# The attention branch as seven quadrant products, and the pooling's moving sums by transfers

## The chip, the cores and the metric

One core of a Trainium2 chip runs the whole block. The metric is the device time of one execution in microseconds (us), the median over the runs shown. Five engines work beside each other, each through its own row of instructions: TensorE (PE, matmuls, with its weight loads as PEld), VectorE (DVE), ScalarE (ACT), GpSimd (POOL) and SyncE (SP), which here only issues transfers (DMAs). An instruction that waits holds up everything behind it in its engine's row.

## The reference

The block mixes a pooling part and an attention part through sigmoid gates, and an MLP follows. All sizes are 1024 (sequence and model), the branches are 512 wide.

```python
def _multiscale_pool(u, w_pool, pool_scale):          # windows w = 2, 4, 8, 16, a group of 128 channels each
    ...
        pooled.append((upper - lower) / count)        # mean over the last min(t + 1, w) rows
    diff = pooled - u
    mixed = jnp.einsum('bsgc,gcd->bsgd', diff, w_pool)
    return mixed.reshape(B, S, POOL_WIDTH) * pool_scale

h = _rmsnorm(x, g_mix_pre[l])
proj = h @ w_in[l] + b_in[l]
u_pool, q, k, v, gates = jnp.split(proj, IN_SPLITS, axis=-1)
y_pool = _multiscale_pool(u_pool, w_pool[l], pool_scale[l])
y_attn = _sliding_window_sink_attention(q, k, v, sinks)   # after a partial rotary embedding
g_pool, g_attn = split(sigmoid(gates))                    # 1024 columns each
merged = g_pool * (y_pool @ w_branch_pool[l]) + g_attn * (y_attn @ w_branch_attn[l])
x = x + _rmsnorm(merged @ w_out[l], g_mix_post[l])
x = x + _rmsnorm(square(relu(_rmsnorm(x, ...) @ w_up[l])) @ w_down[l], ...)
```

## The kernel before

Activations lie with channels on the 128 partitions and the sequence along the free dimension, in tiles of 128x512 or 128x1024. Every product is made in three passes (`PASSES`): each operand is split into a rounded high part and the rest, the high part by a cast on ScalarE (`split`, L101) and the low part by a subtraction on VectorE (L104), and high x high, high x low and low x high are added up in a bank of PSUM. Every matmul of the stages in question is 128x128 by 128x512.

The stages, by TensorE's time in the profile: norms and q, k, v up to 55 us; attention from 55 to 166, with the pooling's input u and the merged pooling weights computed in the gaps of attention; the gates from 166 to 319; the attention branch (L445, L447) to 362; the pooled branch to 406; the output projection to about 490; the MLP to the end.

**Attention.** `others()` is a generator of filler work. For each pooling group gi = 3, 2, 1, 0 it loads weights (`load_u`, `load_wb`, L572 and L582), makes u in two halves (`u_half`), stores u to DRAM (L611), and makes w_pool x w_branch_pool for that group (`wb_half`, stored at L627 to `wbp_dram`). SP also stores attention's output here (`y_dram`, L422), of which POOL adds a second part with an accumulating transfer (L424), and it loads the first gate weights (L475). POOL has small casts and differences of v besides (L103, L104, L330).

**Gates.** The class `Pairs` makes two column tiles of the gates at a time by seven Strassen products on quadrants. `gt.load` brings raw weights, `gt.operand(p, i)` makes the weight operand of product i (a sum or difference on VectorE, then a split). The first products are made from 166 to 210 us, and `rest(p, ...)` makes products 6, 7, 5, 4 and 3 of pair p, 60 matmuls, with an addition on VectorE behind each (L532, L539, L543, L546, L552), the scaling by the norm (L717, L713), the sigmoid on ScalarE (L709) and a store. Product 4 uses the bank of product 7 again, product 3 that of product 5. The operands of pair p are made in front of `rest(p)`.

**Branches.** `branch(w, rhs, base, m)` makes one column tile of 128 channels: a weight load and split, 24 matmuls into two banks (4 x 128 rows, 3 passes, 2 halves of the sequence), and two multiplications by the gates (L932). It runs eight times for attention and eight times for pooling. Attention's moving operand is loaded and split in `load_attn` during the last gate pair. Between the attention branch's tiles, `pool_part(gi)` loads u, adds the bias (L688), makes the moving sums by doubling, one addition of 128x1024 for w = 2 and four for w = 16 (L692, ten in all), subtracts u (L696, L698) and splits the result into `yphi` and `yplo`, the pooled branch's moving operand.

**Order.** Except inside blocks of `tc.manual_schedule`, which keep the order in which the code is written for the engines they name, a scheduler with a cost model orders the rows of PE, DVE and ACT. In attention and the first gates a hand-written interleaving (`fill`, `first`, `second`) decides. Tiles come from pools with a fixed number of buffers (`y`, `x`, `ga`, `bc` and others), so a tile waits until its buffer's last reader is done.

## Time and profile before

| | |
|---|---|
| median of 3 runs | 1109.25 us (1107.92 to 1109.52) |
| profiled execution, own time | 1109.43 us |
| its span | 1107.6 us |
| granted TensorE clock, mean | 0.998 |
| attention with its filler work | 55 to 166.3 us |
| gates: first products, then eight pairs | 166.3 to 209.8, 209.8 to 318.9 us |
| attention branch, pooled branch | 318.9 to 362.4, to 406 us |

The span is the profiled stretch of one execution; the execution's own time is some 2 us longer. Busy time is what an engine spent in instructions, without waits. In a list of groups a row gives line, engine, operation, tiles and count, then busy time and the mean of one in ns, then the idle time ahead of them and what ended it. In a timeline a row gives start and length, and a bracket, where there is one, the idle time before it and its releaser. "PEq", "SPq" and the like are an engine's issuing side.

### The profile page before, as it was taken

What the parts mean: (1) busy time and instruction counts of PE and PEld (TensorE: products, weight loads), DVE (VectorE), ACT (ScalarE), POOL (GpSimd) and SP (SyncE); (2) the same over time, 40 slices, a digit from 0 to 9 for tenths busy, and PEclk for the clock granted to TensorE, in tenths of its full rate; (3) what the DMA queues carried; (4) which work ended last, traced back from release to release, by engine and by line L of the source; (5) the groups of instructions that cost most, each with busy time, mean ns of one, the idle gap of its engine ahead of it and who ended that gap; (6) DMA issues with size and microseconds to landing.
All of it is one profiled execution on the core that took longest, in us unless ns stands there. A gap on an engine that the chain in (4) does not pass through costs nothing.

```text
span 1107.6 us, 13855 instructions
## 1 busy us (share of the span) xinstructions
PE 1097.7 (99%) x5108; PEld 907.5 (82%) x5108; DVE 807.1 (73%) x1175; ACT 547.6 (49%) x916; POOL 62.7 (6%) x107
## 2 busy tenths in 40 slices
PE   9999999999999999999999999999999999999997
PEld 7888788888888888878888888888888888888886
DVE  5578867899768796899878867666548944456596
ACT  7466656444432337587555654444434434344342
POOL 0344220000001120000000000000000000000000
PEclk9999999999999999999999999999999999999999
DMA  9406578355677581570457645445597535534673
GB/s 349 161 11 137 149 169 278 132 191 209 224 256 246 152 186 58 192 271 32 162 197 264 242 169 199 146 151 199 178 371 232 189 98 174 177 102 152 204 229 119
DMA packets 89747, 203.71 MB, mean 184 GB/s; under 512 B 8400, under 2 KB 21072, under 8 KB 89680
## 3 DMA queue, kind: packets, MB, share of 16 engines
q1 hardware_dynamic: 77536, 176.88, 48.0%
q10 hardware_dynamic: 5616, 19.66, 4.6%
q0 software_dynamic: 6528, 6.29, 4.0%
q8 instruction: 40, 0.66, 0.3%
q14 instruction: 27, 0.22, 0.1%
HBM read 147.23 MB, written 55.58 MB: 183 GB/s over the span
## 4 chain that ended last, share of the span: by engine, by line
PE 88%; DVE 5%; DMA 3%; ACT 2%; issue 2%; DVEq 0%; SPq 0%; ACTq 0%
PE mm L511 24%; PE at L511 16%; PE at L1406 16%; PE mm L1406 12%; PE mm L601 4%; PE mm L187 3%; PE mm L445 2%; PE at L196 1%; PE at L419 1%; PE mm L447 1%; PE sc L355 1%; PE sc L187 1%; DMA d<-spill_dram 1%; PE at L1048 1%; PE mm L1048 1%
## 5 line engine op out<-in xcount | busy, mean ns | idle before, releaser
L1406 PE MATMUL at<-ar,wh 128*128 128x512 f32 x744 | 169.6, 389 | 0.0
L1406 PEld LDWEIGHTS at<-ar,wh 128*128 128x128 f32 x744 | 139.6, 188 | 29.3 <-DVE ar L104 0.4
L104 DVE TENSOR_TENSOR wh<-raw,wh 128x1024 fp32r<-128x1024 f32 x53 | 64.8, 1223 | 99.4 <-ACT wh L101 99.4
L1406 PE MATMUL mm<-ar,wh 128*128 128x512 f32 x576 | 131.0, 389 | 0.0
L101 ACT CAST wh<-raw 128x1024 fp32r<-128x1024 f32 x53 | 55.8, 1053 | 146.7 <-PE at L1406 71.6
L1406 PEld LDWEIGHTS mm<-ar,wh 128*128 128x128 f32 x576 | 108.1, 188 | 22.4
L101 ACT CAST wh<-st 128x512 fp32r<-128x512 f32 (+1 forms) x97 | 61.6, 646 | 74.4 <-PE at L511 19.9
L104 DVE TENSOR_TENSOR wh<-st,wh 128x512 fp32r<-128x512 f32 (+1 forms) x97 | 68.8, 719 | 27.8 <-ACT wh L101 25.3
L511 PE MATMUL mm<-gr,wh 128*128 128x512 f32 x333 | 80.4, 391 | 0.0
L511 PEld LDWEIGHTS mm<-gr,wh 128*128 128x128 f32 x333 | 62.1, 188 | 13.1 <-DVE gr L1087 0.4
L511 PE MATMUL mm<-T,wx 128*128 128x512 f32 x288 | 67.6, 389 | 0.0
L511 PEld LDWEIGHTS mm<-T,wx 128*128 128x128 f32 x288 | 54.1, 188 | 11.2
L511 PE MATMUL at<-T,wx 128*128 128x512 f32 x252 | 59.1, 389 | 0.0
L511 PEld LDWEIGHTS at<-T,wx 128*128 128x128 f32 x252 | 47.3, 188 | 9.8
L511 PE MATMUL mm<-x,wh 128*128 128x512 f32 x240 | 55.2, 389 | 0.0
L511 PEld LDWEIGHTS mm<-x,wh 128*128 128x128 f32 x240 | 45.0, 188 | 9.4
L104 DVE TENSOR_TENSOR ar<-B,ar 128x1024 fp32r<-128x1024 f32 x37 | 45.1, 1219 | 4.0 <-ACT ar L101 3.9
L601 PE MATMUL mm<-x,wh 128*128 128x512 f32 x192 | 47.5, 395 | 0.0
L101 ACT CAST ar<-B 128x1024 fp32r<-128x1024 f32 x37 | 38.9, 1051 | 5.9 <-DMA B<-in_w_dn_dram 3.0
L601 PEld LDWEIGHTS mm<-x,wh 128*128 128x128 f32 x192 | 35.3, 188 | 7.7
L511 PE MATMUL at<-gr,wh 128*128 128x512 f32 x150 | 36.7, 390 | 0.0
L101 ACT CAST wx<-ws 128x512 fp32r<-128x512 f32 x30 | 18.6, 620 | 32.7 <-DVE ws L487 17.9
(384 smaller groups left out, 2162.4 us busy)
## 6 DMA issues: line engine op xcount, KB each, us to landing
raw<-f_dram SPq DMA_DIRECT2D x53, 512.0 KB, 3.7
f_dram<-g SPq DMA_DIRECT2D x30, 512.0 KB, 3.3
B<-in_w_dn_dram SPq DMA_DIRECT2D x24, 512.0 KB, 6.3
st<-in_w_up_dram SPq DMA_DIRECT2D x20, 512.0 KB, 4.1
st<-in_w_g_dram SPq DMA_DIRECT2D x18, 512.0 KB, 4.6
f_dram<-g ACTq DMA_DIRECT2D x17, 512.0 KB, 2.6
g<-spill_dram SPq DMA_DIRECT2D x16, 512.0 KB, 5.4
raw<-in_w_dn_dram SPq DMA_DIRECT2D x16, 512.0 KB, 4.7
```

The costliest lines, as they stand in the source:

```text
L101: act.copy(hi, src)
L104: eng.tensor_tensor(lo, src, f32(hi), ALU.subtract)
L187: pe.matmul(bq, xs_[k][n // 4][:, xh, n % 4 * P:(n % 4 + 1) * P], wq[k][:, h, :], start=k == 0 and j == 0, stop=k == NK - 1 and j == 2)
L196: pe.matmul(bkv_of(n), xs_[k][n // 4][:, xh, n % 4 * P:(n % 4 + 1) * P], wkv[k // 2][:, h, k % 2, :], start=k == 0 and j == 0 and not (joi ...
L355: pe.matmul(sb[:, kv, i, :nk], qt[r, qx, m * P:(m + 1) * P], kx[r, k0:k0 + nk], start=j == 0, stop=j == 2)
L419: pe.matmul(flat(yb), v[:, kv, :], flat(p[:, 4 * kv:4 * kv + 4]), start=j == 0, stop=j == len(mms) - 1)
L445: pe.matmul(bs[th], whi[:, k, :], rhs(k, hl, th), start=k == 0 and hl == 0, stop=False)
L447: pe.matmul(bs[th], wlo[:, k, :], rhs(k, 0, th), start=False, stop=k == nk - 1)
L511: pe.matmul(b, w[:, wh, kt, :], xo[kt][:, xh, :], start=not after and kt == 0 and j == 0, stop=kt == 3 and j == 2, skip_group_check=after)
L601: pe.matmul(b, (whi, wlo)[h][:, k, :], xr(k, xh, th), start=j == 0, stop=j == len(mms) - 1)
L1048: pe.matmul(bs[t], gop[i][kt // 2][gh][:, kt % 2, t * P:(t + 1) * P], wop[i][kt // 2][wh][:, kt % 2], start=not after and kt == 0 and j == ...
L1406: pe.matmul(bs[t], fo[fh][:, k2, t * P:(t + 1) * P], wo_[wh][:, k2, :], start=not after and s2 == 0 and k2 == 0 and j == 0, stop=s2 == NS ...
```

## The change

The attention branch is made by a class `Halves` as four weight pairs p of two column tiles, each by seven Strassen products on quadrants (two 128-row tiles of depth, 512 of the sequence). `first(p)` makes products 1 and 2, `rest(p)` makes 5, 6, 3, 7, 4. A product is 2 x 3 = 6 matmuls. The order in time is first(0), first(1), rest(0) with first(2) before its last product, rest(1) with first(3), rest(2), rest(3). In place of two multiplications for a column tile there are seven copies, additions and multiplications on ScalarE and VectorE for a weight pair (L978, L988, L991 copies on ScalarE; L981 to L1003 on VectorE). The moving operand's quadrants are combined on VectorE once (`combine`, L929, T1 to T4, 128x1024 each), and four sums of quadrant weights are made for each weight pair (`weights`, L947 to L950, 128x256 each).

The gates' operands are now made one pair ahead: `rest` calls `side()` after each addition, and a side step makes one operand of pair p + 1; in pairs 4 to 7 the side steps also load, combine and split the branch's operands (table `extra`). SP and POOL keep the written order there.

The pooling's moving sums are made by transfers between DRAM tiles while attention runs: u is stored twice (L619, L620), POOL adds a shifted copy by an accumulating transfer (`shifted`, L597), and for each further doubling SP copies the sum to a new tile first (L677). Eight of the ten additions are done in this way. `pool_load(gi)` then loads u and the sum, two tiles for a group, and `pool_split(gi)` does the remaining doubling, if any, the scaling by 1/w on ScalarE (L709), the subtraction and the split. The pooled branch (`pooled`) takes the first three groups for its first four column tiles before it needs the fourth group.

```diff
+    sum_dram = [[spill[i] for i in rows] for rows in ((20,), (21,), (22, 28), (23, 29, 30, 31))]
...
+    def shifted(gi, i):
+        src = sum_dram[gi][i - 1] if i else u_dram[gi]
+        pool.dma_start(sum_dram[gi][i][:, 1 << i:], src[:, :S - (1 << i)], accum_op=ALU.add)
...
             nc.sync.dma_start(u_dram[gi], u)
+            nc.sync.dma_start(sum_dram[gi][0], u)
...
             yield from u_half(gi, 0)
+            for g, i in {2: ((3, 0),), 1: ((3, 1), (2, 0)), 0: ((3, 2), (2, 1), (1, 0))}.get(gi, ()):
+                shifted(g, i)
...
             yield from u_half(gi, 1)
+            for g, i in {2: ((3, 1),), 1: ((3, 2), (2, 1)), 0: ((3, 3),)}.get(gi, ()):
+                nc.sync.dma_start(sum_dram[g][i], sum_dram[g][i - 1], max_dma_last_dim=4096)
...
-        while step < w:
-            t = place()
-            dve.tensor_tensor(t[:, step:], src[:, step:], src[:, :S - step], ALU.add)
...
+        act.activation(t, t, AF.Identity, bias=bias, scale=1.0 / w)
+        dve.tensor_tensor(u, t, u, ALU.subtract)
...
+    shifted(3, 3)
+    shifted(0, 0)
...
+        PRODUCT = {1: ("A11", "B11"), 2: ("A12", "B21"), 3: ("S4", "B22"), 4: ("A22", "T4"),
+                   5: ("S1", "T1"), 6: ("S2", "T2"), 7: ("S3", "T3")}
...
+        def rest(self, p, sides, between):
+            z, x, t, t2 = zg[self.base, p], self.x.pop(p), self.tmp.pop(p), g32([2, 512])
+            y = self.bank(p)
+            self.mm(y, p, 5)
+            act.copy(t2[:, 0], y)
+            sides[0]()
+            self.mm(x, p, 6, True)
+            act.copy(t[:, 0], x)
+            sides[1]()
+            self.mm(y, p, 3, True)
+            dve.tensor_tensor(t[:, 0], t[:, 0], y, ALU.add)
+            dve.tensor_tensor(z[1][:, 0], z[1][:, 0], t[:, 0], ALU.mult)
+            sides[2]()
+            self.mm(x, p, 7, True)
+            dve.tensor_tensor(t2[:, 0], t2[:, 0], x, ALU.add)
+            dve.tensor_tensor(z[1][:, 1], z[1][:, 1], t2[:, 0], ALU.mult)
+            sides[3]()
+            between()
+            self.mm(x, p, 4, True)
+            dve.tensor_tensor(z[0][:, 1], z[0][:, 1], x, ALU.mult)
...
+        extra = {(4, 2): lambda: w_todo.append(ba.weights(0)),
...
+                 (6, 0): lambda: ba.combine("T1", "B12", "B11", ALU.subtract, "B11"),
...
+        for p in range(4):
...
+            pool_load(p)
...
+            ba.rest(p, (nothing if p < 0 else lambda: w_next(p), nothing, lambda: w_split(p),
+                        lambda: pool_split(p) if p < 3 else None),
+                    (lambda: ba.first(p + 2)) if p < 2 else nothing)
...
+    for m in range(4):
+        pooled(m, range(3))
+    pool_split(3)
```

Lines move by up to some hundred in the changed kernel; a tile's number is its own in each program. SP's row in the second half of attention, before, from the store of the second pooling group to the first load of gate weights (`st<-in_w_g_dram`):

```order
L611 DMA spill_dram<-u_1106 128x1024
L422 DMA y_dram<-yt_1421 256x1x128 x2
L572 DMA st_1579<-in_w_u_dram 128x1024
L627 DMA wbp_dram<-wt_1338 128x8x128
L582 DMA st_1785<-in_w_bp_dram 128x1024
L611 DMA spill_dram<-u_1347 128x1024
L422 DMA y_dram<-yt_1589 256x1x128 x2
L475 DMA st_1875<-in_w_g_dram 128x1024
```

The same stretch of SP's row after; each L677 copies a sum and waits for POOL's accumulation into it:

```order
L620 DMA spill_dram<-u_1106 128x1024
L423 DMA y_dram<-yt_1422 256x1x128 x2
L576 DMA st_1583<-in_w_u_dram 128x1024
L677 DMA spill_dram<-spill_dram 128x1024
L636 DMA wbp_dram<-wt_1339 128x8x128
L677 DMA spill_dram<-spill_dram 128x1024
L586 DMA st_1794<-in_w_bp_dram 128x1024
L619 DMA spill_dram<-u_1348 128x1024
L620 DMA spill_dram<-u_1348 128x1024
L423 DMA y_dram<-yt_1593 256x1x128 x2
L677 DMA spill_dram<-spill_dram 128x1024
L476 DMA st_1887<-in_w_g_dram 128x1024
```

Three copies stand ahead of the first gate weights now, one behind the other.

VectorE's row in gate pair 6, before, from the addition behind product 6 (L532) to the last scaling (L713):

```order
L532 TENSOR_TENSOR z_2800<-z_2800,at_2928 128x512
L104 TENSOR_TENSOR ar_3016<-ws_3006,ar_3016 128x512
L539 TENSOR_TENSOR z_2927<-z_2800,at_2929 128x512
L543 TENSOR_TENSOR z_2927<-z_2927,at_2930 128x512
L546 TENSOR_TENSOR z_2927<-z_2800,at_2929 128x512
L717 TENSOR_TENSOR z_2927<-z_2927,rb_all 128x1024
L552 TENSOR_TENSOR z_2800<-z_2800,at_2930 128x512
L104 TENSOR_TENSOR wh_3166<-st_3163,wh_3165 128x512
L713 TENSOR_TENSOR z_2800<-z_2800,rb_all 128x512
```

The same pair after, to the addition behind product 4 (L548) and the quadrant sum behind it; L533, L541 and L544 are the additions behind products 6, 7 and 5, L929 the branch's quadrant sums, L105 low parts of splits, L492 a weight difference of the next pair:

```order
L533 TENSOR_TENSOR z_2857<-z_2857,at_2975 128x512
L105 TENSOR_TENSOR ar_3032<-ws_2991,ar_3032 128x512
L929 TENSOR_TENSOR q_2939<-q_2939,q_2903 128x1024
L541 TENSOR_TENSOR z_2974<-z_2857,at_2976 128x512
L492 TENSOR_TENSOR st_2859<-st_2859,ws_2991 128x512
L105 TENSOR_TENSOR wo_3081<-q_2964,wo_3080 128x1024
L544 TENSOR_TENSOR z_2974<-z_2974,at_2977 128x512
L105 TENSOR_TENSOR wh_3073<-st_2859,wh_3073 128x512
L105 TENSOR_TENSOR wh_2815<-st_2751,wh_2814 128x1024
L105 TENSOR_TENSOR ar_2817<-ws_2809,ar_2816 128x768
L548 TENSOR_TENSOR z_2974<-z_2857,at_2976 128x512
L929 TENSOR_TENSOR q_2964<-q_2964,q_2939 128x1024
```

Between the additions there now stand up to three operations of the branch's and the next pair's operands; four more rows of the pair follow (two scalings, L728 and L724, the addition L555, and a weight sum L947 of 128x256).

ScalarE's row in the branch, before, with pool_part's bias additions (L688) and the casts of splits (L101):

```order
L101 CAST yphi_3247<-d_3235 128x1024
L688 ACTIVATE d_3285<-d_3285,vec 128x1024
L101 CAST wh_3304<-st_3302 128x512
L688 ACTIVATE d_3378<-d_3378,vec 128x1024
L101 CAST yphi_3294<-d_3285 128x1024
L101 CAST wh_3346<-st_3344 128x512
```

And after, around weight pair 1's products 5 and 6, whose banks L988 and L991 copy out:

```order
L102 CAST wh_3345<-st_3235 128x1024
L701 ACTIVATE d_3241<-d_3241,vec 128x1024
L988 COPY g_3331<-mm_3332 128x512
L709 ACTIVATE d_3242<-d_3242,vec 128x1024
L991 COPY g_3214<-mm_3213 128x512
L102 CAST yphi_3290<-d_3241 128x1024
L701 ACTIVATE d_3327<-d_3327,vec 128x1024
L978 COPY g_3388<-mm_3387 128x512
```

The copies out of banks now stand between the pooling's activations (L701 adds the bias to u, L709 scales the sum).

More of the change, by code (lines that the diff above doesn't have):

```diff
@@ L523, in m2, with rest @@
             self.close_first(self.f0[p][:, :512], b)
-        def rest(self, p, f1, b6, b7, b5, done=(), then=None, b4=None):
+        def rest(self, p, f1, b6, b7, b5, done=(), side=lambda: None, b4=None):
             f0 = self.f0.pop(p)
@@ L532, in rest @@
             dve.tensor_tensor(u2, u2, b6, ALU.add)
+            side()
             if p in self.b1:
@@ L983, in merge, with split_pairs @@
+    gop, wop = {}, {}
+    def split_pairs(srcs, place, behind=None):
+        ops = [(place([2, 512]), place([2, 512])) for _ in srcs]
+        for hi, _ in ops if behind else ():
+            pool.tensor_copy(hi[:, 0, :1], behind[:, 0, :1])
+        for (hi, lo), t in zip(ops, srcs):
+            split(hi, lo, t)
+        return ops
     def merge(j):
@@ L988, in merged, with pooled @@
         return [zg[8, 2 * kh + j][th] for j in range(2)]
-    def x_place(shape):
-        return xp.tile([P] + shape, F32R, tag="x", name=nm("wo"))
+    def pooled(m, ks):
+        if m not in pw:
+            ws = stage([4, P])
+            nc.sync.dma_start(ws, wbp_dram[m])
+            t = wslot([2, 4, P])
+            split(t[:, 0], t[:, 1], ws)
+            tag = "mm" if m in (0, 1, 4, 5) else "at"
+            pw[m] = t, [bank(tag) for _ in range(2)]
+        t, bs = pw[m]
+        for k in ks:
+            for hw, hx in PASSES:
+                for th in range(2):
+                    pe.matmul(bs[th], t[:, hw, k, :], ysp[k][hx][:, th * 512:(th + 1) * 512],
+                              start=k == 0 and hw + hx == 0, stop=k == 3 and hw == 1, skip_group_check=True)
+    pw = {}
+    for m in range(4):
+        pooled(m, range(3))
+    pool_split(3)
+    gate_pair(0, 0)
+    gate_pair(0, 1)
     b11, b12 = merged(0, 1), merged(0, 0)
     for m in range(8):
-        branch(wbp_dram[m], lambda k, hl, th: ysp[k][hl][:, th * 512:(th + 1) * 512], 0, m)
+        if m == 4:
+            gate_pair(0, 2)
+        elif m == 6:
+            gate_pair(0, 3)
+        pooled(m, range(3, 4) if m < 4 else range(4))
+        z = zg[0, m // 2]
+        for th in range(2):
+            dve.tensor_tensor(z[th][:, m % 2], z[th][:, m % 2], pw[m][1][th], ALU.mult)
         if m == 4:
```

208 lines of the change are left out of this document (149 added, 59 removed).

## Prediction

> **What bounds the kernel now.** I read the busy shares first, then TensorE's waits, then the chain of waits, then the busy time stage by stage. The page's head:
>
> ```profile
> span 1107.6 us, 13855 instructions
> PE 1097.7 (99%) x5108; PEld 907.5 (82%) x5108; DVE 807.1 (73%) x1175; ACT 547.6 (49%) x916; POOL 62.7 (6%) x107
> ```
>
> TensorE (PE) is busy for 99% of the span. All its waits together, from the view of waits (total, times, longest), are under 4 us:
>
> ```profile
> PE mm L205 <- DVE zeros L183: 1.5, 1, 1.5
> PE sc L355 <- DVE s L364: 0.8, 2, 0.5
> ...
> PE mm L445 <- ACT wh L101: 0.2, 1, 0.2
> ```
>
> In the chain of waits (start, length) the gate stage is one gapless run of matmuls:
>
> ```profile
> 278.26 13.60 PE mm L511 x60
> 291.86 13.60 PE at L511 x60
> ```
>
> So 60 matmuls of 128x512 take 13.60 us, 0.2267 us each. Removing a matmul here saves that much, as long as the work beside it keeps up. How close that work comes is read by stage (length, then busy time of PE, PEld, DVE, ACT and POOL with counts, clock, DMA share, GB/s):
>
> ```profile
> core 0: us, PE busy (x) PEld busy (x) DVE busy (x) ACT busy (x) POOL busy (x), PEclk, DMA share, GB/s
> 55.00:166.30 111.30, 110.38 (x664) 90.51 (x663) 84.87 (x132) 68.06 (x214) 35.84 (x68) 1.00 0.51 116
> 224.00:308.00 84.00, 84.00 (x372) 69.57 (x371) 72.89 (x108) 38.02 (x51) 0.00 (x0) 1.00 0.65 219
> 306.00:361.50 55.50, 55.50 (x246) 45.96 (x245) 41.81 (x67) 16.11 (x18) 4.16 (x4) 1.00 0.77 247
> ```
>
> The rows are attention, six gate pairs, and the attention branch with the last gate pair. In the gate pairs VectorE is already busy for 87%, in the branch for 75%. The granted clock is 1.00 throughout and the change leaves TensorE as dense, so I leave it there.
>
> **Term 1, the matmuls: -5.44 us.** The attention branch in the groups of the window 318 to 363 us:
>
> ```profile
> L445 PE MATMUL mm<-yahi,wh 128*128 128x512 f32 x64 | 24.9, 389 | 0.0
> L445 PE MATMUL mm<-yalo,wh 128*128 128x512 f32 x64 | 24.9, 389 | 0.0
> L447 PE MATMUL mm<-yahi,wh 128*128 128x512 f32 x64 | 19.7, 389 | 0.0
> ```
>
> That is 192 matmuls. Seven products of six matmuls for each of four weight pairs are 168: 24 x 0.2267 = 5.44 us. The pooled branch keeps 192 (its order alone changes), so this is the only gain on TensorE.
>
> **Term 2, VectorE in the gate pairs: 0.** Durations by shape (busy, mean ns), then four consecutive starts in time:
>
> ```profile
> L104 DVE TENSOR_TENSOR wh<-st,wh 128x512 fp32r<-128x512 f32 x41 | 27.6, 685 | 7.9 <-ACT wh L101 7.7
> L692 DVE TENSOR_TENSOR t<-d 128x1023 f32<-128x1023 f32 x4 | 4.9, 1222 | 3.4 <-ACT d L688 3.4
> L932 DVE TENSOR_TENSOR g<-g,mm 128x512 f32<-128x512 f32 x30 | 19.2, 680 | 3.5 <-PE mm L447 3.5
> ...
> 292.74 1.22 DVE L717 TENSOR_TENSOR z<-z,rb_all 128x1024 f32<-128x1024 f32 x1
> 293.88 0.68 DVE L552 TENSOR_TENSOR g<-g,mm 128x512 f32<-128x512 f32 x1
> 294.47 0.68 DVE L104 TENSOR_TENSOR wh<-st,wh 128x512 fp32r<-128x512 f32 x1
> 295.08 0.68 DVE L713 TENSOR_TENSOR g<-g,rb_all 128x512 f32<-128x512 f32 x1
> ```
>
> Back to back a 1024-wide operation costs 1.14 us and a 512-wide one 0.60; on that line 768 comes to 0.87 and 256 to 0.33 (interpolated). The change puts four quadrant sums (L929), the splits of the branch's operands and of the first weight sums into pairs 4 to 7. The order's piece for pair 6 goes from eight 512s and one 1024, 8 x 0.60 + 1.14 = 5.9 us, to nine 512s, five 1024s, one 768 and one 256: 5.4 + 5.7 + 0.9 + 0.3 = 12.3 us of the pair's 13.60. Counted in the same way the pairs 3 to 7 need 11.4 to 12.9 us. This holds as an average; inside a pair, product 4 reuses the bank that the addition behind product 7 (L541) reads, and product 3 the bank of L544, with one product (12 matmuls, 2.72 us) between. Before, VectorE waited for TensorE at both:
>
> ```profile
> 300.05 0.69 DVE L543 TENSOR_TENSOR z<-z,at 128x512 f32<-128x512 f32 x1 [1.18 <-PE at L511]
> 302.77 0.69 DVE L546 TENSOR_TENSOR z<-z,at 128x512 f32<-128x512 f32 x1 [2.03 <-PE at L511]
> ```
>
> Walking the new order with these durations leaves at least 1.0 us before TensorE waits, least in pair 7. I take 0; bounds 0 and 3 us. The side steps are also what makes the operands one pair early, so none is late at a pair's start.
>
> **Term 3, waits inside the shorter branch: +1.2 us.** The branch now takes 168 x 0.2267 = 38.1 us. VectorE's list for it is 28 merges (28 x 0.60 = 16.8, priced by the L932 row's shape), weight sums and splits about 10, T4's split 1.1, and three pooling groups at two to three 1024s, about 7: 35 us, and it starts some 4 us behind the gates' end by the same walk. It has no slack to speak of, but it can run over: the pooled branch begins with 72 matmuls (16.3 us) that need no merge. The removed moving sums (eight of ten at 1.14, 9.1 us) and the four final combinations are what paid for the room.
>
> What bites is ScalarE, which now copies banks out between TensorE's products and has the pooling's activations queued in the same row. Its prices:
>
> ```profile
> L518 ACT COPY g<-mm 128x512 f32<-128x512 f32 x4 | 2.3, 587 | 3.2 <-PE mm L511 3.2
> L688 ACT ACTIVATE d<-d,vec 128x1024 f32<-128x1024 f32 x4 | 4.6, 1152 | 13.8 <-DMA d<-spill_dram 13.8
> L101 ACT CAST yphi<-d 128x1024 fp32r<-128x1024 f32 x4 | 4.2, 1046 | 8.3 <-DVE d L698 8.3
> ```
>
> For weight pair 1 the row is activation, copy (L988), activation, copy (L991): 1.15 + 0.59 + 1.15 + 0.59 = 3.48 us, while TensorE has two products of six between (2.72): it waits 0.76 us. In pair 2 a cast (1.05) takes an activation's place; part of it is done before, about 0.4 us stays (estimate by the walk). Together 1.2. Bounds: 0, if the activations run ahead, and 4 us, if a pooling load is also late (below).
>
> **Term 4, transfers in attention: 0.** Eight accumulating transfers by POOL (L597), four copies by SP (L677) and four more stores (L620) of 512 KB. What the trace has near (count, KB, us from issue to landing; the first from the branches, the others from the window 85 to 170 us), and the places in time:
>
> ```profile
> s<-in_w_o_dram POOLq DMA_DIRECT2D x8, 512.0 KB, 7.3
> y_dram<-yt POOLq DMA_DIRECT2D x14, 128.0 KB, 5.3
> spill_dram<-u SPq DMA_DIRECT2D x4, 512.0 KB, 3.9
> st<-in_w_g_dram SPq DMA_DIRECT2D x4, 512.0 KB, 4.9
> ...
> 118.89 0.46 POOL L330 TENSOR_TENSOR df<-vf,vf 128x128 f32<-128x128 f32 x1
> 140.19 0.33 SPq L475 DMA_DIRECT2D st<-in_w_g_dram  x1
> 158.67 1.18 ACT L101 CAST wh<-st 128x512 fp32r<-128x512 f32 x2
> 165.00 1.14 ACT L101 CAST wh<-st 128x512 fp32r<-128x512 f32 x2
> 166.13 4.24 PE L511 MATMUL mm<-x,wh 128*128 128x512 f32 x18
> ```
>
> The first accumulation stands behind L330 on POOL, so at 119.4. The first gate weights' load on SP, at 140.19 before, now stands behind the third copy, which needs the third accumulation of the widest group: accumulate, copy, accumulate, copy, accumulate. With A for an accumulation and C for a copy it issues at 119.4 + 3A + 2C. No row shows DRAM to DRAM; A lies between 5.3 and 10 (the 512 KB row with a third on top for the busier queues), C between 3.9 and 8.8 (a store and a load in series). I take A = 7.3, the only accumulation of this size, and C = 4.5, between store and load: 150.3, landing at 155.5, before ScalarE's cast at 158.67. The second load waits for one more accumulation: 157.6, landing at 162.8, before its cast at 165.00. Both hidden, 10 us later than now.
>
> The Trainium skill ("DMA: Bandwidth & Descriptors", section "Anatomy of one DMA — SWDGE (gpsimd) path") gives 2.0 us plus bytes over 436 GB/s for such a transfer, an estimate of 3.2 us for 512 KB. The trace differs, at 7.3; by the page's figure the chain would end some 12 us sooner, and the sum would be the same.
>
> **Term 5, the first gates: +0.3 us.** From 166 to 186 us the loads are what is late, and the transfers are dense:
>
> ```profile
> 178.00:182.00 4.00, 4.00 (x19) 3.30 (x18) 1.59 (x3) 2.61 (x4) 0.00 (x0) 1.00 1.05 406
> 179.39 0.62 ACT L101 CAST wh<-st 128x512 fp32r<-128x512 f32 x1 [3.59 <-DMA st<-in_w_g_dram]
> 183.26 0.62 ACT L101 CAST wh<-st 128x512 fp32r<-128x512 f32 x1 [1.18 <-DMA st<-in_w_g_dram]
> ```
>
> The last extra store and the last accumulations fall here: 0.5 MB is 1.3 us at 406 GB/s for each. The weights cast at 179.39 are used about 182.6, so some 2 us hide. Bounds 0 and 2; I take 0.3, near the lower end.
>
> **Sum.** -5.44 + 0 + 1.2 + 0 + 0.3 = -3.9 us. The profiled run took 1109.43 us (1.8 beside its span), 0.2 above the median of 1109.25, so against the runs: 1109.25 - 3.9 = 1105.3; with the walk's rounding I say 1105.2. I count less than 0.2% (2.2 us) as no change: 1107.0 to 1111.5.
>
> **Rivals.**
> *All hidden.* The copies' rows on ScalarE slide ahead, and the whole 5.44 shows: 1103.8. For it: ScalarE's 16.11 of 55.50 us in the branch. Against: the stack of 3.48 us.
> *The branch eats it.* A pooling load lands late, and the activation that waits for it stands in ScalarE's row ahead of copies that TensorE waits for. The chain of waits of before has one:
>
> ```profile
> 327.24 7.44 DMA d<-spill_dram
> ```
>
> I plan some 4 us; 3.4 us more, once, gives -0.5, 1108.7. For it: the pooling now loads eight tiles there and not four. Against: 2 MB more and 5.4 us less raise the 247 GB/s of the row above to about 315, under the 406 that a row of term 5 shows.
> *VectorE bounds the gate pairs.* If its operations take their full 0.68 and not 0.60, a pair of 12.9 us needs 14.6; three such pairs lose about 1 us each at L541 and L544: 1108.2. For it: the 12.3 of 13.60 us above. Against: 293.88 to 295.08, the starts 0.60 apart.
> *Slower: SP's queue holds the gate weights.* The second load's weights are wanted 12 matmuls after the gates' start, at 168.85; less a cast and a subtraction of 0.62 + 0.68 it must land by 167.5, 5.2 us after its issue. With 119.4 + 4A + 2C, all in series, that needs A under 8.5; from there each us of A costs 4, and the gain of 3.9 is gone at A = 9.4. At A = 11: 4 x 2.5 = 10 us late, 1115.2. For it: the POOL row of 128 KB already takes 5.3 us, and these accumulations read and write DRAM at a shifted, odd address. Against: the second load's extra accumulation overlaps the one ahead of it, which moves the point to A near 10.
> The Trainium skill ("SBUF — State Buffer", section "Who interferes with whom") speaks on this rival's side: transfers issued by GpSimd can starve while VectorE runs its doubled modes. No run here shows it. The trace leaves it open: in attention VectorE is busy for 84.87 of 111.30 us, and its 1024-wide operation costs 1.1 ns an element, no less than the 512-wide one, so no faster mode is seen there.
>
> **Numbers.** Forecast 0.52 (its own range 1104.3 to 1107.0), all hidden 0.13, branch eats it 0.12, VectorE bounds 0.08, SP's queue 0.15. Faster 0.65, same 0.20, slower 0.15. The range runs from 1103.0 (all hidden, less half of the 1.6 us by which the three runs differ) to 1111.0, which leaves out the last rival and little else.
>
> **What would show it.** After: 168 matmuls in the branch, gate pairs of 13.60 us in the chain, TensorE's new waits on ScalarE's copies (L988, L991) near 1 us in total, the gate weights' cast at about 158.7 and gates at 166. Wrong if TensorE waits at the first gates on weights, if L541 or L544 appear among its releasers, or if accumulations take over 8.5 us.

## The result, and the profile after

The changed kernel is slower: 1118.3 us (1115.82 to 1120.95, four runs) against 1109.38 (four runs), a ratio of 1.0082, 95% interval 1.0054 to 1.0111. I had forecast 1105.2, in a range that ended at 1111.0. The profiled execution is the lowest of the four, 1115.82 us with a span of 1114.0 against 1107.6, so 6.4 us of the 9 can be read from its trace.

TensorE's waits, which were under 4 us together before, have a new row after, by far the largest (the page's head, then that row of the view of waits):

```profile
span 1114.0 us, 13850 instructions
PE mm L512 <- ACT wh L102: 6.2, 2, 3.6
```

The chain of waits of after shows the place, at the gates' start, and behind it a dense stage as before:

```profile
159.84 14.68 DMA st<-in_w_g_dram
...
180.52 10.82 DMA st<-in_w_g_dram
...
235.31 13.60 PE mm L512 x60
```

The full gate pairs begin at 235.31 us instead of 223.86: 11.45 us lost in all. Of it 0.9 is there when the gates start (167.04 against 166.13), and nearly all of that since the first 10 us of the span, long before any changed instruction. From the gates' start to the first full pair it was 57.73 us before and is 68.27 now. TensorE's rows of after there, and the granted clock in the stretches behind its two waits (last columns: clock, DMA share, GB/s):

```profile
167.04 5.60 PE L512 MATMUL mm<-x,wh 128*128 128x512 f32 x24
175.27 13.20 PE L512 MATMUL mm<-x,wh 128*128 128x512 f32 x48 [2.62 <-ACT wh L102]
192.03 13.14 PE L512 MATMUL mm<-x,wh 128*128 128x512 f32 x49 [3.57 <-ACT wh L102]
...
175.27:178.00 2.73, 2.73 (x7) 2.11 (x8) 2.41 (x4) 1.99 (x3) 0.00 (x0) 0.50 1.06 255
192.03:200.00 7.97, 7.97 (x28) 6.12 (x29) 5.60 (x9) 3.74 (x7) 0.00 (x0) 0.80 1.05 344
```

The two waits are 6.19 us. The 48 matmuls behind the first took 13.20 us instead of 48 x 0.2267 = 10.88, the first 49 behind the second 13.14 instead of 11.11: another 4.35 us. Together that is 10.54 us, all of 68.27 - 57.73: the waits and the slower matmuls behind them are the whole loss. The granted clock, 0.50 over 2.73 us behind the first wait and 0.80 over 7.97 us behind the second, makes 0.50 x 2.73 + 0.20 x 7.97 = 3.0 us of the 4.35. The other 1.4 us are not the clock: in the run of plain shifted copies below it stayed at 1.00, and the 120 matmuls behind the wait there took 28.02 us instead of 27.20 (row in the last section). What makes these gaps was not looked into.

The branch itself does what the forecast said, in the windows of after for the gate pairs, the branch and the pooled branch:

```profile
235.31:330.50 95.19, 95.19 (x421) 78.82 (x421) 88.19 (x129) 43.86 (x56) 0.00 (x0) 1.00 0.61 218
330.50:368.60 38.10, 38.10 (x169) 30.97 (x168) 35.34 (x56) 24.00 (x32) 2.43 (x2) 1.00 0.74 244
```

TensorE is busy for all of 38.10 us, beside 35.34 us of VectorE. From the full pairs to the first MLP products in the chain of waits it was 492.81 - 223.86 = 268.95 us before and is 499.21 - 235.31 = 263.90: 5.05 us gained.

Why the weights came late, in SP's row of after (start, length of the issue), in ScalarE's casts that waited, and, last, in SP's row of before:

```profile
150.20 0.55 SPq L476 DMA_DIRECT2D st<-in_w_g_dram  x1
155.75 0.83 SPq L476 DMA_DIRECT2D st<-in_w_g_dram  x1
159.84 0.58 SPq L476 DMA_DIRECT2D st<-in_w_g_dram  x1
164.89 5.60 SPq L476 DMA_DIRECT2D st<-in_w_g_dram  x1
172.52 6.04 SPq L619 DMA_DIRECT2D spill_dram<-u  x1
...
165.91 1.14 ACT L102 CAST wh<-st 128x512 fp32r<-128x512 f32 x2
174.60 1.14 ACT L102 CAST wh<-st 128x512 fp32r<-128x512 f32 x2 [6.57 <-DMA st<-in_w_g_dram]
191.36 0.62 ACT L102 CAST wh<-st 128x512 fp32r<-128x512 f32 x1 [7.98 <-DMA st<-in_w_g_dram]
...
170.71 0.95 SPq L475 DMA_DIRECT2D st<-in_w_g_dram  x1
```

The two loads I had walked went out at 150.20 and 155.75 and were in time. The third goes out at 159.84, about when it did before, and takes 14.7 us to land, where the load took 4.9 before. Issuing itself takes 5.60 us at 164.89 and 6.04 at 172.52, so SP's queue is backed up. The fifth load, on which the second wait hangs, is late mainly because it went out late: at 180.52, where it went out at 170.71 before. SP spent most of the time between on the two long issues. Its landing took 10.8 us against 8.7.

The two queues' share of the 16 transfer engines from 110 to 200 us, before and then after (q1 is SP's, q0 POOL's; packets, MB, share):

```profile
q1 hardware_dynamic: 10199, 15.48, 54.5%
q0 software_dynamic: 3260, 1.57, 16.6%
...
q1 hardware_dynamic: 10924, 18.14, 58.8%
q0 software_dynamic: 4416, 5.76, 40.5%
```

POOL's queue grows by 24 points of 90 us, 21.5 us for the eight accumulations, about 2.7 us each of all 16 engines. With SP's it is 99% of the stretch, where it was 71%.

### The profile page after: what moved, and what is told of

Its sections match the earlier page's. It is cut to its first block, busy times and chain, and to the rows that moved or that the text cites. A ratio compares the mean times of both kernels' runs of the same rounds, so it can differ in the third digit from the quotient of the medians.

```text
span 1114.0 us, 13850 instructions
## 1 busy us (share of the span) xinstructions
PE 1097.6 (99%) x5084; PEld 905.4 (81%) x5084; DVE 821.0 (74%) x1190; ACT 564.0 (51%) x935; POOL 64.2 (6%) x113
## 4 chain that ended last, share of the span: by engine, by line
PE 89%; DVE 4%; DMA 3%; ACT 2%; issue 1%; SPq 0%; DVEq 0%; ACTq 0%
PE mm L512 23%; PE at L512 16%; PE at L1594 16%; PE mm L1594 12%; PE mm L609 3%; PE mm L188 3%; DMA st<-in_w_g_dram 2%; PE at L1165 2%; PE mm L1165 2%; PE mm L967 2%; PE at L967 2%; PE at L197 1%; PE sc L356 1%; PE sc L188 1%; PE at L420 1%
## 5 line engine op out<-in xcount | busy, mean ns | idle before, releaser
L105 DVE TENSOR_TENSOR wh<-raw,wh 128x1024 fp32r<-128x1024 f32 x53 | 64.8, 1224 | 100.0 <-ACT wh L102 99.8
L102 ACT CAST wh<-raw 128x1024 fp32r<-128x1024 f32 x53 | 55.8, 1052 | 146.5 <-PE at L1594 62.0
L105 DVE TENSOR_TENSOR wh<-st,wh 128x512 fp32r<-128x512 f32 (+1 forms) x94 | 69.0, 744 | 40.7 <-ACT wh L102 38.3
L102 ACT CAST wh<-st 128x512 fp32r<-128x512 f32 (+1 forms) x94 | 61.2, 664 | 66.6 <-DMA st<-in_w_g_dram 18.8
L512 PE MATMUL mm<-x,wh 128*128 128x512 f32 x240 | 59.5, 406 | 6.3 <-ACT wh L102 6.2
L512 PEld LDWEIGHTS mm<-x,wh 128*128 128x128 f32 x240 | 46.6, 196 | 18.3 <-ACT wh L102 7.6
L609 PE MATMUL mm<-x,wh 128*128 128x512 f32 x192 | 47.5, 395 | 0.0
L105 DVE TENSOR_TENSOR ar<-B,ar 128x1024 fp32r<-128x1024 f32 x37 | 45.1, 1220 | 2.6 <-ACT ar L102 2.2
L102 ACT CAST ar<-B 128x1024 fp32r<-128x1024 f32 x37 | 38.9, 1052 | 4.9 <-DVE B L1569 2.8
L102 ACT CAST wx<-ws 128x512 fp32r<-128x512 f32 x30 | 18.6, 620 | 33.2 <-DVE ws L488 17.9
```

Source lines behind the costliest of these rows:

```text
L102: act.copy(hi, src)
L105: eng.tensor_tensor(lo, src, f32(hi), ALU.subtract)
L512: pe.matmul(b, w[:, wh, kt, :], xo[kt][:, xh, :], start=not after and kt == 0 and j == 0, stop=kt == 3 and j == 2, skip_group_check=after)
L609: pe.matmul(b, (whi, wlo)[h][:, k, :], xr(k, xh, th), start=j == 0, stop=j == len(mms) - 1)
```

## The experiments

Theory A: the accumulations' engine time around 150 to 195 us makes the gate loads late, and nothing else is wrong. Rivals: another part of the change loses; SP's own extra stores and copies, or its waiting for POOL, are the cause. The kernel before ran again on the same chip beside each of them (medians of 1108.9 to 1109.5 us); ratios are to those runs.

**Strassen alone.** The transfers undone, all moving sums on VectorE:

```diff
-            nc.sync.dma_start(sum_dram[gi][0], u)
...
-                shifted(g, i)
...
-                nc.sync.dma_start(sum_dram[g][i], sum_dram[g][i - 1], max_dma_last_dim=4096)
...
-        w, bias, step = WINDOWS[gi], ..., 1 << len(sum_dram[gi])
+        w, bias, step = WINDOWS[gi], ..., 1
```

> The changed kernel with its transfers undone: no second store of u, no accumulations, no copies; all ten moving sums on VectorE in the branches, from a second load of u (same output). Theory A, that the transfers made the whole loss and the branch's 24 matmuls show nearly in full: the first gates have no waits on weights, gates end near 319 us as before, and the time is 1104 to 1106. Rival R, that the loss or part of it comes from elsewhere in the change (VectorE in the gate pairs, the branch's order): 1109 or more. A third outcome: eight more additions of 1.14 us, 9.1 us, on VectorE in a branch of 38 us make TensorE wait there, 1106 to 1112 with waits at the branch or the pooled tiles and none at the first gates.

1115.74 us, ratio 1.0057 (1.0040 to 1.0074). The gates start on time, with no wait on weights. TensorE waits instead at the branch (0.6 us) and at the pooled tiles (4.3 and 2.3 us, L1153), and the clock falls behind those waits:

```profile
PE mm L1153 <- ACT yphi L101: 4.3, 1, 4.3
...
380.00:412.00 32.00, 29.63 (x112) 23.54 (x112) 31.04 (x36) 10.93 (x13) 8.14 (x9) 0.87 0.69 190
```

VectorE is busy for 31.04 of 32 us there. So the third outcome holds, larger than I put it: the transfers were needed, and undoing them costs 10 us (1115.74 against the 1105.61 of the run without accumulations below) at another place.

**Transfers alone.** The kernel before, with the transfers and the new `pool_in` (t is the sum, loaded):

```diff
+            nc.sync.dma_start(sum_dram[gi][0], u)
...
+                shifted(g, i)
...
+                nc.sync.dma_start(sum_dram[g][i], sum_dram[g][i - 1], max_dma_last_dim=4096)
...
-        for _ in pool_in(gi, u, y_place):
...
+        pool_in(gi, u, t)
```

> The kernel before with the transfers alone: u stored twice, eight accumulations, four copies, the pooling loads the sum; the branch as 192 matmuls (same output). Theory A: the same late gate loads as in the changed kernel, some 10 us of waits and slow matmuls between 167 and 200 us, and nothing gained in the branch: 1118 to 1121. Rival R: 1109 to 1111.

1122.11 us, ratio 1.0111 (1.0096 to 1.0127): 13 us lost, slightly more than forecast, with the waits of the changed kernel (7.0 us in two waits on the same casts, L102).

**No accumulations,** stores and copies kept:

```diff
-                shifted(g, i)
```

> The changed kernel without the eight accumulating transfers; the second stores of u and SP's four copies stay (the sums are left out, so the pooling's values are others). Theory A1, that the accumulations are what fills the transfer engines: the gate loads land in 5 to 7 us, and the time is 1104 to 1106. Theory A2, that SP's own extra transfers (4 MB of copies and stores ahead of the loads in SP's queue) are it: the copies run earlier now, but waits of 4 us or more stay at the first gates, 1108 to 1115.

1105.61 us, ratio 0.9963 (0.9950 to 0.9977). No wait on weights; the load lands in a median of 5.0 us, with 19.7 MB in SP's queue between 110 and 200 us, more than in any kernel above (15.5 before):

```profile
q1 hardware_dynamic: 11358, 19.68, 66.7%
```

A1 holds, A2 falls: SP's copies and stores alone make no wait. It is also the kernel that the forecast's sum described, and it is in the forecast's range.

**No copies,** all accumulations kept, so SP waits for none:

```diff
-                nc.sync.dma_start(sum_dram[g][i], sum_dram[g][i - 1], max_dma_last_dim=4096)
...
-        pool.dma_start(sum_dram[gi][i][:, 1 << i:], src[:, :S - (1 << i)], accum_op=ALU.add)
+        pool.dma_start(sum_dram[gi][0][:, 1 << i:], u_dram[gi][:, :S - (1 << i)], accum_op=ALU.add)
```

> The changed kernel with all eight accumulations, but without SP's four copies: each accumulation adds u at its shift to the group's one sum tile (other values in the pooling). SP waits for no accumulation any more. Theory A1, accumulations fill the engines: loads of 10 us and more stay around 160 to 190 us, 1112 to 1118. Theory A2, copies and what they hold up on SP: the loads issue as before at 140, 147 and 159 us and land in 5 to 8 us, 1104 to 1107.

1110.91 us, ratio 1.0018 (1.0008 to 1.0028): between the two expectations. SP's queue carries less than in the run above, yet the fourth and fifth gate loads take 11.8 and 9.7 us (4.3 and 8.7 before) and TensorE waits 3.6 us. The fifth also goes out 5.7 us later than before (176.45 against 170.71):

```profile
PE mm L512 <- ACT wh L102: 3.6, 1, 3.6
...
164.67 11.77 DMA st<-in_w_g_dram
176.45 9.72 DMA st<-in_w_g_dram
```

So transfers of another queue delay the loads, and what stands ahead of them in SP's queue did not do it by itself in the run above. The Trainium skill ("DMA: Bandwidth & Descriptors", section "Queues, rings and completion order") says that each transfer engine takes turns between the queues that have work for it, packet by packet. These two runs agree with it.

But the accumulations without the copies cost only 5.3 us (1110.91 less the 1105.61 without accumulations) of the 12.7 that the changed kernel lost by them (1118.3 less 1105.61). The other 7.4 us come only with SP's copies and SP's waits for POOL beside them. No run separates these two.

**Plain shifted copies** on POOL in place of accumulations:

```diff
-        pool.dma_start(sum_dram[gi][i][:, 1 << i:], src[:, :S - (1 << i)], accum_op=ALU.add)
+        pool.dma_start(sum_dram[gi][i][:, 1 << i:], src[:, :S - (1 << i)])
```

> The changed kernel with POOL's eight transfers as plain shifted copies, without the addition (the sums are left out, other values in the pooling): the same bytes of payload, queue, order and waits. Theory A1a, that an accumulation costs the transfer engines more than a copy (its target is read too, some 2.8 us of all 16 engines each against about 1.2 for a copy, from the queues' shares of the kernels measured so far): 8 x 1.6 = 13 us of engine time less, and most of the waits at the first gates go: 1105 to 1108. Theory A1b, that it is the POOL queue's transfers as such, or the chain of waits between the queues: 1112 or more.

1108.56 us, ratio 0.9988 (0.9977 to 0.9998), a little above A1a's range. POOL's queue takes less time for the same bytes:

```profile
q0 software_dynamic: 3904, 5.76, 29.0%
```

The 11.5 points under the accumulations' 40.5 are 10.4 us of 90, 1.3 us for each transfer: about half of what an accumulation takes. The plain copies also land sooner (medians of 6.0 to 7.5 us by size, against 7.6 to 9.7), so SP's row waits less; this run doesn't tell the two apart. With the copies and SP's waits kept, 2.9 us (1108.56 less 1105.61) of the 12.7 are left. One wait of 2.2 us on a gate cast remains.

**The chain in the gate pairs 0 to 4,** one or two accumulations in each:

```diff
+            for g, i in {0: ((3, 0),), 1: ((3, 1),), 2: ((3, 2), (0, 0)), 3: ((3, 3), (2, 0)), 4: ((2, 1), (1, 0))}.get(p, ()):
+                if i:
+                    nc.sync.dma_start(sum_dram[g][i], sum_dram[g][i - 1], max_dma_last_dim=4096)
+                shifted(g, i)
```

> The changed kernel with all eight accumulations and four copies moved from attention into the gate pairs 0 to 4 (one or two accumulations in each 13.6 us), where the transfers are busy for about 0.6 of the time; same output. Theory A (the stretch from 150 to 200 us is over its transfer capacity, and nothing else is wrong with them): no waits at the first gates, 1104 to 1106. Rival: 23 us of engine time in 68 us at a share of 0.6 fills that stretch as well, and raw weights or the stores of the gates come late there: 1108 or more, with waits on operands (ACT or DVE rows of splits) in pairs 1 to 5.

1123.63 us, ratio 1.0134 (1.0114 to 1.0153). No waits at the first gates, but one long one in the pairs, and SP's row shows why:

```profile
PE at L512 <- DVE z L541: 14.7, 1, 14.7
...
249.87 0.50 SPq L1084 DMA_DIRECT2D spill_dram<-spill_dram  x1
263.70 0.47 SPq L1084 DMA_DIRECT2D spill_dram<-spill_dram  x1
278.50 0.52 SPq L934 DMA_DIRECT2D st<-in_w_ba_dram  x1
```

SP runs ahead of TensorE, so each copy waits for an accumulation just issued, 13.8 us from one copy to the next. The raw weights of the branch stand behind the fourth copy and go out only at 278.50 us; VectorE waits 16.4 us for them (L941), and TensorE behind it. This is the rival's outcome by another mechanism, the one that I had feared for the first gates. As a test of capacity it says nothing.

**The first four accumulations only,** the other four sums on VectorE:

```diff
-    sum_dram = [[spill[i] for i in rows] for rows in ((20,), (21,), (22, 28), (23, 29, 30, 31))]
+    sum_dram = [[spill[i] for i in rows] for rows in ((), (), (22,), (23, 29, 30))]
...
```

> The changed kernel with only the accumulations (3,0), (3,1), (3,2) and (2,0) by transfers, those issued before 150 us; the other four moving sums on VectorE in the branch, with their stores and copies gone; same output. Theory A: half of the engine time is gone and all of it lies early, so waits at the first gates are 0 to 2 us; VectorE in the branch has 4 x 1.14 = 4.6 us more. 1105 to 1109. If waits as in the whole change remain (6 us and slow matmuls behind them), it is the early accumulations that push the loads back: 1112 or more.

1108.97 us, ratio 0.9998 (0.9988 to 1.0007). No wait at the gates; the four sums on VectorE cost the gain at the branch and behind it (1.7, 1.0, 0.5 and 0.3 us of waits on VectorE).

**The sums on GpSimd,** no transfers:

```diff
-            dve.tensor_tensor(n[:, step:], t[:, step:], t[:, :S - step], ALU.add)
+            pool.tensor_tensor(n[:, step:], t[:, step:], t[:, :S - step], ALU.add)
```

> The changed kernel without the transfers, and the ten moving sums as additions on GpSimd in place of VectorE; same output. GpSimd's 128x128 addition takes 0.46 us; at 0.15 us fixed and the rest by length a 1024-wide one would take 2.6 us, ten of them 26 us of the branch's 38. If that holds and VectorE is not slowed beside it: 1104 to 1107. If the chain of four additions of the last group, over 10 us, or a slower VectorE comes late for the pooled tiles: 1108 to 1118, with waits at the pooled tiles as with the sums on VectorE.

1118.03 us, ratio 1.0081 (1.0066 to 1.0096). GpSimd's additions are as quick as hoped, but VectorE is slower beside them (see the last section), and TensorE waits 3.1, 2.6, 1.6 and 0.8 us.

**The last four accumulations later.** Same work, but (3,3), (2,1), (1,0) and (0,0) wait for a gate product:

```diff
-            for g, i in {2: ((3, 0),), 1: ((3, 1), (2, 0)), 0: ((3, 2), (2, 1), (1, 0))}.get(gi, ()):
+            for g, i in {2: ((3, 0),), 1: ((3, 1), (2, 0)), 0: ((3, 2),)}.get(gi, ()):
...
-    shifted(3, 3)
-    shifted(0, 0)
...
+        pool.tensor_copy(small()[:, :1], gt.f0[5][:, 512:513])
+        for g, i in ((3, 3), (2, 1), (1, 0), (0, 0)):
+            shifted(g, i)
```

> The changed kernel with nothing taken away: the same eight accumulations, but the last four on POOL, (3,3), (2,1), (1,0) and (0,0), wait for the first gate product of pair 5 (near 191 us, by a copy of one column of its result), so they run at 190 to 224 us, where the transfers' share was 0.3 to 0.4 without them; same output. Theory A (only the stretch of 150 to 195 us is over its transfer capacity): gates start without waits on weights and none come later, since pair 5's loads need little; the time is that of the kernel without accumulations, 1103 to 1107. Rival B (the four early accumulations alone, with the stores and copies, already push the third and fourth gate loads back): waits of 2 to 6 us stay at the first gates, 1108 to 1114. Rival C: the four at 190 to 224 us delay the raw weights of the first gate pairs: waits on ACT or DVE splits in pairs 0 and 1.

1108.08 us, ratio 0.9990 (0.9978 to 1.0002). 10 us better than the changed kernel, by the time of four transfers alone. A wait of 1.6 us on a gate cast remains in the profiled execution: rival B, in its small form. (That execution took 1110.45 us, above the median.)

**Their stores and copies later too:** four copies on SP ahead of two loads of raw weights.

```diff
+                for g, i in ((3, 3), (2, 1), (1, 0), (0, 0)):
+                    nc.sync.dma_start(sum_dram[g][i], sum_dram[g][i - 1] if i else u_dram[g], max_dma_last_dim=4096)
                 gt.load(2)
                 gt.load(3, g32([NK, P]))
```

> The changed kernel with its last four accumulations and, in addition, their second stores and copies (as four copies on SP behind the loads of the first gates' weights, near 195 to 205 us) out of the stretch of 145 to 190 us: in it stay the four accumulations issued up to 148 us and nothing else new; same output. Theory A, that engine time between 150 and 190 us is what costs: 4 MB of stores and copies and four accumulations less there leave no waits on weights at the first gates, and the time is that of the kernel without accumulations: 1104 to 1107. Rival B, that the four early accumulations alone push the gate loads: a wait of 1 to 2 us stays, 1107 to 1110. Rival C, that the moved ones now come late themselves (SP waits at the copies, raw weights of gate pair 0 and 1 late): waits in the first pairs, 1108 or more.

1111.82 us, ratio 1.0025 (1.0014 to 1.0036). The first gates have no wait now, but something comes late in pair 0, at a share of 1.05:

```profile
PE at L512 <- ACT ar L102: 4.1, 1, 4.1
...
223.71 0.69 DVE L541 TENSOR_TENSOR z<-z,at 128x512 f32<-128x512 f32 x1 [4.89 <-DMA spill_dram<-z]
...
210.00:224.00 14.00, 11.58 (x50) 8.83 (x48) 8.42 (x15) 4.89 (x9) 0.23 (x1) 1.00 1.05 276
```

Rival C's time came, but not by late raw weights. VectorE's addition behind product 7 (L541) waits 4.89 us for a store of the gates (L865, from ScalarE's queue), and the operand that TensorE waits for stands behind it in VectorE's row. The two stores go out from 215.24 us and land in 8.3 and 10.2 us. The raw weights of pair 1, at 201.62 and 202.00, are slow too (9.8 and 13.2 us), but VectorE's first use of them (L485, at 218.13) doesn't wait.

**The copies behind those two loads:**

```diff
                 gt.load(3, g32([NK, P]))
+                for g, i in ((3, 3), (2, 1), (1, 0), (0, 0)):
+                    nc.sync.dma_start(...)         # the same four copies
```

> The kernel before this one (last four accumulations, with their copies, out of the stretch of 145 to 190 us), but the four copies on SP stand behind the two loads of raw weights for gate pairs 0 and 1 and not ahead of them; same output. In the run before, the copies went out at 197.7 us, the loads behind them at 201.6, and SP's next load only at 217, so the copies have 15 us of an otherwise idle SP. Theory A: no waits on weights at the first gates and none in pairs 0 and 1; 1104 to 1107, the time of the kernel without accumulations. Rival C2: any 23 us of transfers in 200 to 224 us delay the stores and loads around them, wherever they stand in SP's row: a wait of 2 us or more in pairs 0 to 2, 1108 to 1112.

1112.22 us, ratio 1.0026 (1.0016 to 1.0036). Theory A's form here was wrong. The raw weights of pair 1 land in under 5 us now, but the two stores of the gates, from 215.30 us, meet the accumulations issued from 209 to 214, land in 9.6 and 12.9 us, and VectorE waits for the first again:

```profile
225.01 0.69 DVE L541 TENSOR_TENSOR z<-z,at 128x512 f32<-128x512 f32 x1 [6.14 <-DMA spill_dram<-z]
...
PE at L512 <- ACT ar L102: 5.4, 1, 5.4
```

The chain of waits names a load issued at 217.10 here, and I took it for the cause in the next expectation. But it brings raw weights of pair 2, and VectorE was held by L541 until 225.6.

**The copies near 185 us,** behind the loads for the first products and ahead of the raw weights of pair 0:

```diff
                 gt.load(2 * p + 10)
+                if p == 2:
+                    for g, i in ((3, 3), (2, 1), (1, 0), (0, 0)):
+                        nc.sync.dma_start(...)     # the same four copies
```

> As in the two runs before (the last four accumulations with their copies moved out of 145 to 190 us), but the four copies stand on SP ahead of the raw weights of gate pair 0, near 185 us, so that copies and accumulations fall into 185 to 215 us; the load whose weights were late twice goes out at 217 us, behind them; same output. Theory A (transfers cost only where a load with little slack is under way): no wait at the first gates, none in pair 0 and 1, and the time of the kernel without accumulations, 1104 to 1107, which would be faster than both kernels. Rival C2 (23 us of transfers more do not fit anywhere between 150 and 224 us): a wait of 2 us or more at 190 to 230 us, 1108 to 1112.

1104.88 us (1104.06 to 1105.55), ratio 0.9959 (0.9946 to 0.9973): faster than both kernels, with all eight accumulations in place. The copies go out at 186.04 and the last accumulation at 196.39. The stores of the gates that were late twice go out from 214.53 and land in 2.6 and 3.6 us, and L541 doesn't wait:

```profile
186.04 2.58 SPq L899 DMA_DIRECT2D spill_dram<-spill_dram  x4
196.39 0.82 POOL L597 DMA_DIRECT2D spill_dram<-spill_dram  x1 [0.24 <-issue]
214.53 0.93 ACTq L865 DMA_DIRECT2D spill_dram<-z  x2
...
166.00:200.00 34.00, 34.00 (x152) 28.15 (x151) 27.28 (x43) 20.60 (x36) 5.34 (x6) 1.00 1.00 316
```

The changed kernel's row for the same window shows what the same work cost there:

```profile
166.00:200.00 34.00, 27.71 (x106) 21.03 (x105) 16.06 (x25) 13.28 (x25) 5.72 (x6) 0.90 1.11 319
```

A share of 1.00 did no harm here. The two first gate loads, at 140.59 and 147.17 beside the early accumulations, took 9.7 and 11.9 us to land, and TensorE waited for neither. That is theory A with a sharper point than I began with: the accumulations' engine time costs where it meets a transfer with little slack, be it a load or a store whose tile is wanted again, and not where a stretch is full.

## Why the prediction was wrong, step by step

The step that failed is term 4, "transfers in attention: 0" ("Both hidden"), with term 5, "+0.3", behind it: 0.3 us was forecast for both together, and the stage lost 10.5.

- *Issue times in term 4: right.* 150.3 was forecast for the first load, 150.20 came. The second went out at 155.75, forecast 157.6. An accumulation took 8.3 us to land (5.2 to 10.8), forecast 7.3 for A; a copy 4.9, forecast 4.5. The hit at 150.20 has some luck in it: with the medians the formula gives 119.4 + 3 x 8.3 + 2 x 4.9 = 154.1, but the first accumulation went out at 120.24, and the three in the chain were quicker than the median (about 6.6, 5.2 and 7.7 us from issue to the copy or load behind them).

```profile
DMA to landing us min/median/max: 5.2/8.3/10.8
DMA to landing us min/median/max: 4.2/4.9/6.3
```

- *The rest of term 4: wrong.* I priced the transfers only by what waits for them, as a chain, and gave the loads their old 4.9 us to land. What they take from other transfers was left out: 2.7 us of all engines each, in a stretch whose row in the prediction already had 0.51 on average, and 1.07 at its end (160 to 166 us before). The third load, which I did not walk, landed in 14.7 us.
- *Term 5: the place right, the size wrong.* It counted 1.3 us for each of "the last extra store and the last accumulations", as 0.5 MB at 406 GB/s, and ended its bounds at 2 us. An accumulation takes twice that, half of it because it is no plain copy (the run of plain shifted copies). And what counts is whom it delays, which no share of 0.5 MB shows.
- *What no term had:* the clock. 4.35 of the 10.5 us are slower matmuls behind the waits, 3.0 of them by the granted clock. I left the clock alone since TensorE would stay dense.
- *The rival "SP's queue holds the gate weights"* had the sign and the size (slower, 1115.2 at A = 11), but not the mechanism: the chain was in time (150.20 and 155.75), and without the copies, where SP waits for no accumulation, 3.6 of 6.2 us of waits and 5.3 of 12.7 us were left. What the rival has right is that SP's row held a load back: the fifth, by long issues and not by the chain. Its chance of 0.15 was for a chain.
- *Term 1: right.* The 24 matmuls show in full: 38.10 us for the branch, forecast 38.1.
- *Term 2: right.* The gate pairs are gapless at 13.60 us with VectorE busy for 88.19 of 95.19 us. The rival that VectorE bounds them didn't come.
- *Term 3: forecast +1.2, measured 0.* No row of waits names L988 or L991. ScalarE's stack for weight pair 1 runs back to back, with the starts 1.05, 0.47 and 1.05 us apart (and TensorE's row for products 6 and 3):

```profile
346.30 1.14 ACT L701 ACTIVATE d<-d,vec 128x1024 f32<-128x1024 f32 x1
347.35 0.56 ACT L988 COPY g<-mm 128x512 f32<-128x512 f32 x1
347.82 1.15 ACT L709 ACTIVATE d<-d,vec 128x1024 f32<-128x1024 f32 x1
348.87 0.57 ACT L991 COPY g<-mm 128x512 f32<-128x512 f32 x1
...
346.73 2.92 PE L967 MATMUL mm<-gr,ar 128*128 128x512 f32 x12
```

  It takes 3.1 us and not the 3.48 of the added durations, and ends at 349.44; product 7 begins at 349.49. I had used starts for VectorE and durations for ScalarE. That alone would leave 0.4 us of wait above the 2.72; the rest is that the first activation began at 346.30, before product 6 (346.73).
- *The sum without the accumulations* is 1105.61 us, forecast 1105.2. That it comes so close is partly luck: term 3 did not come, so term 1 alone would give 1103.8, which its profiled execution has (1103.90), and its runs go from 1102.94 to 1107.03. Room for the transfers was there too, some 10 to 36 us later (the last run).

Left open: why the changed kernel's other runs are up to 5 us above the profiled one (their traces weren't taken), how the 7.4 us divide that the accumulations cost only with the copies beside them, and how the 1.6 us of wait that remain with the last four accumulations later divide between stores and copies.

## What to carry to other kernels

A transfer has two prices: how long its own reader waits, and how much of the engines it takes from loads that others wait for. Before moving arithmetic into transfers, add up their engine time in each stage's window beside the share that is there, and walk every load and store in that stage with little slack, in every queue, not only those behind the new instructions in their row. When a change both gains and loses, run its halves: here each half alone lost, and moving four accumulations and their copies by 10 to 36 us turned 9 us lost into 4 us gained.

## What the runs showed of the hardware

- An accumulation from DRAM to DRAM of 512 KB took about 2.7 us of all 16 transfer engines, a plain shifted copy in the same queue about 1.4 (2.7 less 1.3). It took as much where the transfers had more room: in the run with the chain in the gate pairs POOL's queue has 18.3% of the 200 us from 110 to 310, before 7.5%, which is 2.7 us each.
- A wait of 2.62 us in TensorE was followed by 2.73 us at a granted clock of 0.50; the wait of 2.2 us in the run of plain shifted copies left it at 1.00 (window of that run, and the matmuls behind the wait):

```profile
166.00:200.00 34.00, 31.84 (x138) 25.46 (x137) 23.59 (x36) 18.50 (x33) 5.20 (x6) 1.00 0.95 318
185.75 28.02 PE L512 MATMUL mm<-x,wh 128*128 128x512 f32 x120 [2.16 <-ACT wh L102]
```

  The Trainium skill ("TensorE: Matmul & The Clock Gate", section "What's actually happening") has half clock after an idle window of about 3.4 us; the measurement decides, and here 2.6 us was enough.
- In the run with the sums on GpSimd, a VectorE addition with both inputs in SBUF (`g<-g,g`) that began during a GpSimd addition took 1.59 to 2.38 us instead of 0.68 (four times: at 351.07, 354.43, 362.66 and 366.81 us). One that began just before a GpSimd addition (at 340.63, against 340.79) took 0.68. An addition with one input in PSUM (`g<-g,mm`) took 0.68 during a GpSimd addition too (at 366.10, beside the one of 365.17):

```profile
340.63 0.68 DVE L983 TENSOR_TENSOR g<-g,g 128x512 f32<-128x512 f32 x1
362.66 2.38 DVE L983 TENSOR_TENSOR g<-g,g 128x512 f32<-128x512 f32 x1
366.10 0.68 DVE L986 TENSOR_TENSOR g<-g,mm 128x512 f32<-128x512 f32 x1
...
362.41 2.08 POOL L694 TENSOR_TENSOR t<-d 128x1023 f32<-128x1023 f32 x1 [1.78 <-DMA d<-spill_dram]
365.17 2.76 POOL L694 TENSOR_TENSOR t<-t 128x1022 f32<-128x1022 f32 x1
```
